# Head-major cumulated decays in DRAM, and the substitution's initial values loaded ahead of the diagonal blocks

## The chip, the cores and the metric

The kernel runs on one core of a Trainium2 chip. The metric is the device time of one launch in microseconds (us), the median of three runs. All engines of the core work side by side: TensorE (PE, with its weight loads as PEld), VectorE (DVE), ScalarE (ACT), GpSimd (POOL) and SyncE (SP), which here issues all DMA transfers, in one queue in order.

## What is computed

One decoder layer for a sequence of S = 1024 rows of D = 1024 columns, in float32: a gated delta rule with 8 heads and sparse attention in parallel, merged, then an MLP. The change touches the delta rule. Per head, with a chunk of 64 rows (cut from the reference):

```python
g_cum = jnp.cumsum(g, axis=-1)                      # g: log decay, <= 0
diff = g_cum[..., :, None] - g_cum[..., None, :]
decay = jnp.where(incl, jnp.exp(jnp.where(incl, diff, 0.0)), 0.0)
k_beta = k * beta[..., None]
a_mat = jnp.where(strict, jnp.einsum('bhnid,bhnjd->bhnij', k_beta, k) * decay, 0.0)
lhs = a_mat + jnp.eye(C, dtype=f32)
sol = lax.linalg.triangular_solve(lhs, rhs, left_side=True, lower=True, unit_diagonal=True)
...
o = ... lax.scan(step, state0, xs)                  # state carried over the chunks
...
o_gdn = rms_norm(o_gdn, gdn_norm_g) * silu(z)
```

The kernel takes chunks of 128 rows, 8 of them (b = 0 to 7), and inverts each chunk's unit lower triangle of 128 x 128: diagonal blocks of 32 x 32 by substitution, then joins of blocks to 64 and to 128.

## The kernel before

**The planner.** The program is written as many small chains (generators). An object of class `Weave` runs them: it keeps an estimate of when each engine comes free, takes at every step the chain of the best priority that is ready by that estimate, and lets it issue up to its next `yield`. A chain can yield a named event, as `("zu", 3)`, and is not taken up before another chain has announced it. What is issued is fixed: `wv.issue` ties each instruction to the one issued before it on its engine. So the order on each engine is decided by estimates when the program is built, and on the chip every engine works through its own order, with waits where data are late. The time on the chip doesn't feed back into the order. All instructions are recorded by one helper, so the profile gives them all line 2105 (2106 after the change); they are told apart by the names of their tiles.

**The stage of the heads**, from 270 to 980 us. `gdense` (priority 9, the last) computes the projections of the heads' q, k, v and of the gates in units of 128 columns: for each of two halves 24 matmuls `dd` of 128x512 in three passes, so 48 to a unit. These dd are what fills PE between the heads' own work. The first dd of a unit's half waits for the event `("drained", u - 1, half)`: the unit before must have been copied out of PSUM. For a q, k or v that is done by `conv(u)`, the causal convolution, with ACT's copy into `cu` (two buffers); and `conv(u)` waits until the convolution before the last one is done:

```python
if len(convs) > 1:
    yield ("conv", convs[-2])
...
A_.activation(cu[:, 3 + half * HALF:3 + (half + 1) * HALF], cus[u, half], AF.Copy)
wv.done("drained", u, half)
```

A convolution is one product on ACT, three on DVE (`qt<-cu,vecs,qt`), ACT's `cu<-qt` and a last product on DVE (`qt<-cu,qt`).

**A head h** then goes through these chains:
- `keys(h)`: es, the cumulated decays of the head, is read from the DRAM tile GC into all 128 partitions; PE transposes kt (`tt<-ident,kt`); ACT makes `es` = exp(−|es − own decay|); PE multiplies kt with itself, DVE makes the triangle `am`.
- Then, still in `keys`: four stores bring am's diagonal blocks to DRAM (`ZA<-am`), four loads bring them back in another layout into `um` (`um<-ZA`); `sx` is loaded with the initial values `c_xinit`, after the event `("zu", h - 1)` because sx has one buffer; POOL runs 31 steps of substitution, two operations each (`stmp<-sx,um` and `sx<-sx,stmp`); four stores (`ZU<-sx`) and four loads (`um<-ZU`) put the inverses into um, and between them stands `wv.done("zu", h)`.
- `join(h)`: DVE transposes blocks (`t<-um`), PE makes small products of 32 x 32 and 64 x 64 (`jj`), ACT copies between them (`ys`, `t`, `y`, `um`).
- `scan(h)`: over the chunks PE's `cc` and `oo`, DVE's `sr`, `sst` and `vv<-oo`, ACT's `svn`.
- `output(h)`: DVE's small operations on `fe`, `fo`, `fot` (a reciprocal root), `vv<-vv,fo`, PE's `tt<-ident,vv`, a product with the gate, a store.

Meanwhile DVE and ACT count for the attention's selection of keys (`tkeq`, `tkcm`, with `cand` and `thr`). Behind the heads the attention opens: SP loads `ql`, PE transposes it (`s<-ident,ql`), ACT and DVE split it into `qh` and `qlo`, PE makes the scores (`s<-kTh,qh` and the like). `misc_post`, ahead of the stage, computes the cumulated decays gc and stores them to GC.

Of the kernel before, what the change touches and what calls it, by code (L numbers as in the profile page):

```python
# [9 lines left out]
F32 = mybir.dt.float32  # L10
# [10 lines left out]
P = 128  # L21
S = 1024
D = 1024
NB = S // P
KT = D // P
HALF = 512
H = 8
# [22 lines left out]
def body(tc, a, out, dbg=None):  # L50
# [4 lines left out]
    def pool(name, bufs=1, side=None, space=None):  # L55
        kw = {}
        if space is not None:
            kw["space"] = space
        elif side is not None:
            kw["side"] = side  # L60
        if space is not DRAM:
            kw["reuse_waits"] = "tile"
        es = ExitStack()
        p = es.enter_context(tc.tile_pool(name=name, bufs=bufs, **kw))
        return p, es
# [16 lines left out]
    dr, dr_es = pool("dr", space=DRAM)  # L82
# [15 lines left out]
    V_, A_, G_, PE_, SY_ = (wv.engine(e, n) for e, n in ((V, "V"), (A, "A"), (G, "G"), (PE, "PE"), (SY, "SY")))  # L98
# [21 lines left out]
    ident = cst.tile([P, P], F32, name="ident")  # L120
# [20 lines left out]
    kng = ix.tile([P, P], F32, name="kng")  # L141
    QD = dr.tile([S, H * P], F32, name="QD")
    KD = dr.tile([S, 2 * P], F32, name="KD")
    GC = dr.tile([H * NB, P], F32, name="GC")
    XD = dr.tile([S, D], F32, name="XD")
    VD = dr.tile([S, 2 * P], F32, name="VD")
    xs, vrow = [], scp.tile([P, P], F32, name="tkcm")
# [135 lines left out]
    def dense():  # L283
        jobs = [(0, 0), (1, 0), (0, 1), (1, 1), (1, 2)]
        jobs += [(u, t) for u in range(2, len(units)) for t in range(3 if u == 2 else 4)]
        for u, t2 in jobs:
# [3 lines left out]
            if u == 0:  # L290
                if t2 == 0:
                    outs[u] = ix.tile([P, S], F32, name="misc")
                    wv.add(1, misc_post())
                ps = pd.tile([P, HALF], F32, name="dd")
                n = 0
                for k in range(KT):
                    yield ("ht", t2, k)
                    h_, l_ = hi[k], lo[k]
                    for l, r in ((h_, ht_hi[k][t2]), (h_, ht_lo[k][t2]), (l_, ht_hi[k][t2])):
                        PE_.matmul(ps, l, r, start=n == 0, stop=n == 3 * KT - 1)  # L300
                        n += 1
                        yield 0.0
                wv.add(1, drain(outs[u][:, t2 * HALF:(t2 + 1) * HALF], ps, ("half", t2)))
                if t2:
                    wv.done("pdense", u)
                continue
# [46 lines left out]
    def col(name, pl=cst):  # L353
        return pl.tile([P, NB, H], F32, name=name)

    c64 = lambda t: t.rearrange("p b h -> p (b h)")
    gx, gt, gu, gl_, gd = (col(n, ix) for n in ("gx", "gt", "gu", "gl_", "gd"))
    aexp = cst.tile([P, H], F32, name="aexp")
    beta = col("beta")
    gc, ngc, eg, egl, egd = (col(n) for n in ("gc", "ngc", "eg", "egl", "egd"))  # L360
# [4 lines left out]
    def misc_post():  # L365
# [59 lines left out]
        pg = p1.tile([P, 4, P], F32, name="tp")  # L425
        PE_.matmul(pg[:, 0, :64], triu, c64(gl_), start=True, stop=True)
        PE_.matmul(pg[:, 1, :64], ones, c64(gl_), start=True, stop=True)
        yield
        V_.tensor_copy(c64(gc), pg[:, 0, :64])
        V_.tensor_scalar(c64(ngc), pg[:, 0, :64], -1.0, None, op0=OP.mult)  # L430
        A_.activation(c64(egl), pg[:, 1, :64], AF.Exp)
        yield
# [2 lines left out]
        yield  # L435
        A_.activation(egd, egd, AF.Exp)
        pg = p1.tile([P, 4, P], F32, name="tp")
        PE_.transpose(pg[:64, 0, :], c64(gc), ident)
        yield
        gr = ix.tile([64, P], F32, name="gt")  # L440
        V_.tensor_copy(gr, pg[:64, 0, :])
        yield
        SY_.dma_start(GC, gr)


    scores = {qb: mkp.tile([P, (qb + 1) * P], F32, name=f"sc{qb}") for qb in range(2, NB)}
# [309 lines left out]
    def conv(u):  # L756
# [35 lines left out]
        wv.done("conv", u)  # L792
        st[h][c + "t"] = o
        wv.add(2, {"k": keys, "q": queries, "v": values}[c](h))


    def keys(h):
# [4 lines left out]
        es = gp.tile([P, NB, P], F32, name="es", bufs=2)  # L802
        am = gq.tile([P, NB, P], F32, name="am", bufs=2)
        um = gp.tile([P, NB, P], F32, name="um", bufs=2)
        kss = gp.tile([P, NB], F32, name="kss", bufs=2)
        SY_.dma_start(es, GC.rearrange("(b h o) p -> h o b p", h=H, o=1)[h].to_broadcast([P, NB, P]))
        dma = ("es", h)
        after(dma)
        for half in range(2):
# [5 lines left out]
            for i in range(4):  # L815
                b = half * 4 + i
# [28 lines left out]
        for half in range(2):  # L845
            yield tt.ready
            ps, slot_ = tt.get()
            for i in range(4):
                b = half * 4 + i
                PE_.matmul(ps[:, i, :], blk(kt, b), blk(kt, b), start=True, stop=True)  # L850
            yield
            for i in range(4):
                b = half * 4 + i
# [10 lines left out]
        st[h].update(kd=kd, aq=es, am=am, av=av, nb=nb_, um=um)  # L864
        wv.done("keys", h)

        for q in range(4):
            SY_.dma_start(ZA[h][:, q].rearrange("n r c -> r n c"),
                          am[32 * q:32 * q + 32, :, 32 * q:32 * q + 32])
        yield  # L870
        sa = um.rearrange("p n c -> p (n c)").rearrange("p (r c) -> p r c", r=32)
        for r in range(4):
            SY_.dma_start(sa[32 * r:32 * r + 32], ZA[h].rearrange("n q r c -> (n q) r c"))
        sx = gq.tile([P, 8, 32], F32, name="sx", bufs=1)
        stmp = gq.tile([P, 8, 32], F32, name="stmp", bufs=1)
        if h:
            yield ("zu", h - 1)
        SY_.dma_start(sx, a["c_xinit"])
        yield
        for j in range(31):  # L880
            w, m = j // 4 + 1, 31 - j
# [9 lines left out]
        zu = ZU[h].rearrange("(n q) k r c -> q (k r) n c", q=4)  # L891
# [205 lines left out]
    gq, gq_es = pool("gq", side="right")  # L1097
# [1079 lines left out]
```

## Time and profile before

| | |
|---|---|
| median of 3 runs | 1871.73 us (1867.83 to 1872.14) |
| the profiled execution | 1870.41 us, its span 1868.7 us |
| mean granted TensorE clock | 0.985 of full speed |
| busy: PE, PEld | 1819.1 us (97%), 1548.2 us (83%) |
| busy: DVE, ACT, POOL | 1261.8 us (68%), 1026.4 us (55%), 531.7 us (28%) |

The profile is one execution, read by the hardware profiler; all durations below are from it. Busy PE is matmuls only, and its ends are modelled, since matmuls overlap in the array; the distance from one start to the next is the better measure. The granted clock is given as a share of the full 2.4 GHz: 0.50 is the lower level of 1.2 GHz, and a figure between them is a mean over a stretch with both. An idle time behind an instruction names its releaser: what the instruction had waited for last.

### The profile page before, as it was taken

How to read it: one execution, taken by the hardware profiler on the slowest of the kernel's cores; microseconds unless marked ns; L12 is line 12 of the kernel's file. 1: busy time of each engine (PE TensorE's matmuls, PEld its weight loads, DVE VectorE, ACT ScalarE, POOL GpSimd, SP SyncE). 2: the span in 40 equal slices, each digit the busy share in tenths (PEclk: the TensorE clock that was granted, in tenths of full speed). 3: DMA queues.
4: the chain of work that ended last, by engine and by line, in shares of the span. 5: the costliest groups of instructions: out<-in, count | busy, mean ns of one | idle time of the engine just before them, and what ended most of it. 6: DMA issues, size and time to landing. Idle time of an engine off the chain costs nothing.

```text
span 1868.7 us, 28344 instructions
## 1 busy us (share of the span) xinstructions
PE 1819.1 (97%) x10214; PEld 1548.2 (83%) x10214; DVE 1261.8 (68%) x2606; ACT 1026.4 (55%) x2262; POOL 531.7 (28%) x751
## 2 busy tenths in 40 slices
PE   8999999999999979999999999999999999999999
PEld 7889998887888868888887788877888888888887
DVE  4557758767768797654347767677766667957655
ACT  6556647756664544553236666666766665333330
POOL 0223640650543146154003211131232222222210
PEclk8999999998999989999999999999999999999999
DMA  4102232312332222222327322221544549463323
GB/s 160 46 25 67 69 114 62 83 44 63 53 79 48 55 67 72 66 63 66 99 95 237 121 80 68 80 96 63 203 158 141 167 160 343 140 198 102 124 79 135
DMA packets 197822, 195.70 MB, mean 105 GB/s; under 512 B 36609, under 2 KB 148658, under 8 KB 197682
## 3 DMA queue, kind: packets, MB, share of 16 engines
q1 hardware_dynamic: 197682, 193.89, 33.8%
q8 instruction: 80, 1.31, 0.3%
q14 instruction: 60, 0.49, 0.1%
HBM read 139.69 MB, written 54.17 MB: 104 GB/s over the span
## 4 chain that ended last, share of the span: by engine, by line
PE 91%; DVE 5%; ACT 3%; DMA 1%; issue 1%; SPq 0%; POOL 0%; DVEq 0%; ACTq 0%; POOLq 0%
PE dd L2105 53%; PE o L2105 15%; PE s L2105 7%; PE pt L2105 6%; PE tt L2105 3%; PE cc L2105 2%; PE jj L2105 2%; PE sq L2105 2%; PE oo L2105 1%; DVE w L2105 1%; DVE rqs L2105 1%; DVE pr L2105 1%; PE tp L2105 0%; DVE sc L2105 0%; DMA pj<-in_x_dram 0%
## 5 line engine op out<-in xcount | busy, mean ns | idle before, releaser
L2105 PE MATMUL dd<-hh,w 128*128 128x512 f32 x1568 | 522.4, 404 | 2.4 <-ACT cu L2105 1.5
L2105 PEld LDWEIGHTS dd<-hh,w 128*128 128x128 f32 x1568 | 292.1, 190 | 55.5 <-ACT cu L2105 2.2
L2105 PE MATMUL dd<-hl,w 128*128 128x512 f32 x784 | 317.2, 405 | 0.6 <-DVE hl L2105 0.6
L2105 PE MATMUL dd<-w,hh 128*128 128x256 f32 x960 | 182.4, 287 | 0.0
L2105 ACT ACTIVATE m<-m 128x512 f32<-128x512 f32 (+1 forms) x240 | 139.8, 624 | 74.5 <-PE dd L2105 31.5
L2105 PE MATMUL dd<-hh,m 128*128 128x512 f32 x520 | 172.1, 396 | 1.9 <-DVE w L2105 1.6
L2105 PEld LDWEIGHTS dd<-hl,w 128*128 128x128 f32 x784 | 149.2, 190 | 26.8 <-DVE hl L2105 1.5
L2105 DVE TENSOR_TENSOR m<-m,m 128x512 fp32r<-128x512 f32 (+2 forms) x177 | 134.8, 789 | 36.2 <-ACT m L2105 32.7
L2105 PEld LDWEIGHTS dd<-w,hh 128*128 128x128 f32 x960 | 154.4, 194 | 1.6
L2105 POOL TENSOR_TENSOR stmp<-sx,um 128x60 f32<-128x60 f32 (+24 forms) x248 | 111.8, 451 | 98.1 <-DMA sx<-in_c_xinit_dram 79.9
L2105 PE MATMUL dd<-w,hl 128*128 128x256 f32 x480 | 137.3, 286 | 0.0
L2105 PEld LDWEIGHTS dd<-hh,m 128*128 128x128 f32 x520 | 97.1, 189 | 22.0 <-DVE w L2105 1.8
L2105 DVE TENSOR_SCALAR_CACHE_REDUCE tkeq<-sc,cand 128x384 f16<-128x384 f32 (+3 forms) x128 | 103.4, 808 | 1.5
L2105 POOL TENSOR_TENSOR m<-m,m 128x512 f32<-128x512 f32 x48 | 67.6, 1415 | 126.7 <-ACT m L2105 63.3
L2105 PE MATMUL dd<-hl,m 128*128 128x512 f32 x260 | 102.5, 394 | 0.0
L2105 POOL TENSOR_TENSOR sx<-sx,stmp 128x60 f32<-128x60 f32 (+24 forms) x248 | 96.8, 390 | 19.4
L2105 PEld LDWEIGHTS dd<-w,hl 128*128 128x128 f32 x480 | 93.1, 194 | 0.1
L2105 ACT ACTIVATE ha<-m 128x1024 fp32r<-128x1024 f32 x43 | 43.8, 1055 | 80.0 <-PE s L2105 33.8
L2105 DVE TENSOR_TENSOR w<-w,w 128x1024 fp32r<-128x1024 f32 (+1 forms) x56 | 64.7, 1160 | 25.8 <-ACT w L2105 25.6
L2105 ACT ACTIVATE hh<-m 128x1024 fp32r<-128x1024 f32 x40 | 40.7, 1054 | 75.1 <-PE o L2105 37.6
L2105 PE MATMUL o<-hh,m 128*128 128x512 f32 x248 | 80.3, 391 | 0.0
L2105 ACT ACTIVATE tkcm<-sc,cand 128x896 f16<-128x896 f32 x64 | 69.9, 1093 | 17.4 <-DVE cand L2105 12.9
(460 smaller groups left out, 4427.5 us busy)
## 6 DMA issues: line engine op xcount, KB each, us to landing
HD<-m SPq DMA_DIRECT2D x106, 256.0 KB, 2.3
m<-HD SPq DMA_DIRECT2D x53, 512.0 KB, 3.9
w<-in_w_in_dram SPq DMA_DIRECT2D x48, 512.0 KB, 3.9
m<-in_w_mlp_up_dram SPq DMA_DIRECT2D x33, 512.0 KB, 5.0
wraw<-in_w_in_dram SPq DMA_DIRECT2D x8, 1024.0 KB, 5.2
m<-in_w_mlp_down_dram SPq DMA_DIRECT2D x16, 512.0 KB, 4.5
w<-in_x_dram SPq DMA_DIRECT2D x10, 512.0 KB, 4.7
hh<-in_w_mlp_down_dram SPq DMA_DIRECT2D x10, 512.0 KB, 5.0
```

Of the source, the lines that this page charges most:

```text
L2105: ins = f(*args, **kw)
```

## The change

Two edits. The DRAM tile GC gets a row of 1024 numbers for each head, where it had a row of 128 for each pair of chunk and head. For that gc is copied once more on DVE, into `gx` with the heads outermost, gx is transposed instead of gc, and the store goes to the new layout. A head's es is then read as one piece of 4 KB for each partition, where it was eight of 512 B. In `keys`, the wait for `("zu", h - 1)` and the load of sx now stand ahead of the ZA stores and the um loads; so these too come behind `("zu", h - 1)`.

```diff
--- before.py
+++ after.py
@@ -141,7 +141,7 @@
     kng = ix.tile([P, P], F32, name="kng")
     QD = dr.tile([S, H * P], F32, name="QD")
     KD = dr.tile([S, 2 * P], F32, name="KD")
-    GC = dr.tile([H * NB, P], F32, name="GC")
+    GC = dr.tile([H, S], F32, name="GC")
     XD = dr.tile([S, D], F32, name="XD")
     VD = dr.tile([S, 2 * P], F32, name="VD")
     xs, vrow = [], scp.tile([P, P], F32, name="tkcm")
@@ -427,6 +427,7 @@
         PE_.matmul(pg[:, 1, :64], ones, c64(gl_), start=True, stop=True)
         yield
         V_.tensor_copy(c64(gc), pg[:, 0, :64])
+        V_.tensor_copy(c64(gx).rearrange("p (h b) -> p b h", h=H), pg[:, 0, :64].rearrange("p (b h) -> p b h", h=H))
         V_.tensor_scalar(c64(ngc), pg[:, 0, :64], -1.0, None, op0=OP.mult)
         A_.activation(c64(egl), pg[:, 1, :64], AF.Exp)
         yield
@@ -435,12 +436,12 @@
         yield
         A_.activation(egd, egd, AF.Exp)
         pg = p1.tile([P, 4, P], F32, name="tp")
-        PE_.transpose(pg[:64, 0, :], c64(gc), ident)
+        PE_.transpose(pg[:64, 0, :], c64(gx), ident)
         yield
         gr = ix.tile([64, P], F32, name="gt")
         V_.tensor_copy(gr, pg[:64, 0, :])
         yield
-        SY_.dma_start(GC, gr)
+        SY_.dma_start(GC.rearrange("h (b p) -> (h b) p", p=P), gr)
 
 
     scores = {qb: mkp.tile([P, (qb + 1) * P], F32, name=f"sc{qb}") for qb in range(2, NB)}
@@ -803,7 +804,7 @@
         am = gq.tile([P, NB, P], F32, name="am", bufs=2)
         um = gp.tile([P, NB, P], F32, name="um", bufs=2)
         kss = gp.tile([P, NB], F32, name="kss", bufs=2)
-        SY_.dma_start(es, GC.rearrange("(b h o) p -> h o b p", h=H, o=1)[h].to_broadcast([P, NB, P]))
+        SY_.dma_start(es.rearrange("p b c -> p (b c)"), GC[h:h + 1, :].to_broadcast([P, S]))
         dma = ("es", h)
         after(dma)
         for half in range(2):
@@ -864,18 +865,18 @@
         st[h].update(kd=kd, aq=es, am=am, av=av, nb=nb_, um=um)
         wv.done("keys", h)
 
-        for q in range(4):
-            SY_.dma_start(ZA[h][:, q].rearrange("n r c -> r n c"),
-                          am[32 * q:32 * q + 32, :, 32 * q:32 * q + 32])
-        yield
-        sa = um.rearrange("p n c -> p (n c)").rearrange("p (r c) -> p r c", r=32)
-        for r in range(4):
-            SY_.dma_start(sa[32 * r:32 * r + 32], ZA[h].rearrange("n q r c -> (n q) r c"))
         sx = gq.tile([P, 8, 32], F32, name="sx", bufs=1)
         stmp = gq.tile([P, 8, 32], F32, name="stmp", bufs=1)
         if h:
             yield ("zu", h - 1)
         SY_.dma_start(sx, a["c_xinit"])
+        for q in range(4):
+            SY_.dma_start(ZA[h][:, q].rearrange("n r c -> r n c"),
+                          am[32 * q:32 * q + 32, :, 32 * q:32 * q + 32])
+        yield
+        sa = um.rearrange("p n c -> p (n c)").rearrange("p (r c) -> p r c", r=32)
+        for r in range(4):
+            SY_.dma_start(sa[32 * r:32 * r + 32], ZA[h].rearrange("n q r c -> (n q) r c"))
         yield
         for j in range(31):
             w, m = j // 4 + 1, 31 - j
```

The count of every kind of instruction on every engine stays the same, but for one DVE copy more. The orders of all engines are alike up to the heads' stage at about 387 us, and again from the attention's later part on (about 1290 us); between, the planner has set them anew. On SP, head 1 went before: ZA(1), a weight load, um<-ZA(1), ZU(0), a weight load, um<-ZU(0), sx; after: ZU(0), a weight load, um<-ZU(0), sx, ZA(1), um<-ZA(1), and ZU(1) comes one weight load later. Three places are shown, on PE and once on DVE.

**The unit boundary at 613 us.** The names dd<-hh and dd<-hl are the dense matmuls; a new second name behind them (w_6543 and w_6544, then w_6718) marks the next unit. Before, on PE:

```order
L2105 MATMUL dd<-hh_110,w_6544 128x512
L2105 MATMUL dd<-hh_112,w_6543 128x512
L2105 MATMUL dd<-hl_113,w_6543 128x512
L2105 MATMUL dd<-hh_112,w_6544 128x512
L2105 MATMUL jj<-um,am 64x64 x8
L2105 MATMUL tt<-ident,kt 128x128 x4
L2105 MATMUL jj<-y_6911,t_6786 64x64 x8
L2105 MATMUL cc<-vv,um 128x128
L2105 MATMUL cc<-svn,kd 128x128
L2105 MATMUL oo<-svn,es 128x128
L2105 MATMUL tt<-ident,vv 128x128 x4
L2105 MATMUL dd<-hh_98,w_6718 128x512
```

After; the last oo of the scan of head 2 stands four rows above these:

```order
L2106 MATMUL dd<-hh_110,w_6489 128x512
L2106 MATMUL dd<-hh_112,w_6488 128x512
L2106 MATMUL tt<-ident,kt 128x128 x4
L2106 MATMUL dd<-hl_113,w_6488 128x512
L2106 MATMUL dd<-hh_112,w_6489 128x512
L2106 MATMUL tt<-ident,kt 128x128 x4
L2106 MATMUL tt<-ident,vv 128x128 x4
L2106 MATMUL jj<-um,am 32x32 x16
L2106 MATMUL tt<-ident,vv 128x128 x4
L2106 MATMUL jj<-ys,t_6886 32x32 x16
L2106 MATMUL jj<-t_6886,ys 32x32 x8
L2106 MATMUL dd<-hh_98,w_6654 128x512
```

Before, 21 dd lay between the end of that scan and the boundary, where the pile of joins, scan and transposes stands; after, 7 lie there, and the pile is 4 groups of transposes and 40 joins. What DVE has to do in the same time begins after the change with these rows, of which the first is that scan's last `vv<-oo`:

```order
L2106 TENSOR_TENSOR vv<-oo,sqs 128x128
L2106 TENSOR_SCALAR tkeq,cnt<-sc_141,cand 128x512
L2106 TENSOR_TENSOR nxt<-nxt,thr 128x1
L2106 TENSOR_SCALAR fe<-qss 128x8
L2106 TENSOR_SCALAR tkeq,cnt<-sc_142,cand 128x640
L2106 TENSOR_TENSOR nxt<-nxt,tki 128x1
L2106 SCALAR_TENSOR_TENSOR fe<-oss,fe 128x8
L2106 TENSOR_SCALAR tkeq,cnt<-sc_143,cand 128x768
L2106 TENSOR_TENSOR thr<-thr,nxt 128x1
L2106 TENSOR_SCALAR fo<-fe 128x8
L2106 TENSOR_SCALAR tki<-cnt 128x4
L2106 SCALAR_TENSOR_TENSOR qt<-cu,vecs,qt 128x1024
```

Behind them follow, in the same order of DVE, one product of w, two more `qt<-cu,vecs,qt`, the other small fo and fot, `vv<-vv,fo`, a memset, three transposes `t<-um`, one `kt<-tt` and `qt<-cu,qt`. Moved ahead of the last product are the memset, the transposes and the `kt<-tt`; the count over 384 columns, which came behind `vv<-oo` before, now stands ahead of it.

**The unit boundary at 655 to 668 us**, the end of the scan of head 3 (a `cc`, `oo` each for the state and for the new values). Before, on PE:

```order
L2105 MATMUL cc<-svn,kd 128x128
L2105 MATMUL oo<-svn,es 128x128
L2105 MATMUL dd<-hh_112,w_6927 128x512
L2105 MATMUL cc<-sst,kt 128x128
L2105 MATMUL oo<-sst,qt 128x128
L2105 MATMUL cc<-sr,um 128x128
L2105 MATMUL oo<-svn,es 128x128
L2105 MATMUL tt<-ident,kt 128x128 x8
L2105 MATMUL tt<-ident,vv 128x128 x4
L2105 MATMUL dd<-hh_98,w_7174 128x512
L2105 MATMUL dd<-hl_99,w_7174 128x512
L2105 MATMUL tt<-ident,vv 128x128 x4
```

After, the same boundary, where w_7193 ends and w_7376 begins; the scan of head 3 is under way here:

```order
L2106 MATMUL oo<-svn,es 128x128
L2106 MATMUL dd<-hl_111,w_7193 128x512
L2106 MATMUL dd<-hh_110,w_7194 128x512
L2106 MATMUL dd<-hh_112,w_7193 128x512
L2106 MATMUL dd<-hl_113,w_7193 128x512
L2106 MATMUL dd<-hh_112,w_7194 128x512
L2106 MATMUL dd<-hh_98,w_7376 128x512
L2106 MATMUL tt<-ident,kt 128x128 x4
L2106 MATMUL dd<-hl_99,w_7376 128x512
L2106 MATMUL dd<-hh_98,w_7377 128x512
L2106 MATMUL dd<-hh_100,w_7376 128x512
L2106 MATMUL dd<-hl_101,w_7376 128x512
```

Before, two rounds of the scan, eight transposes of kt and four of vv stand with no dd between them. After, dd stand between all rows of the scan, its last oo comes 43 dd behind this boundary, and the first transposes of vv another 58 dd behind that.

**The opening of the attention at 982 us.** Before, on PE:

```order
L2105 MATMUL dd<-hl_105,w_10601 128x512
L2105 MATMUL dd<-hh_104,w_10602 128x512
L2105 MATMUL s<-ident,ql 128x128 x4
L2105 MATMUL dd<-hh_106,w_10601 128x512
L2105 MATMUL dd<-hl_107,w_10601 128x512
L2105 MATMUL dd<-hh_106,w_10602 128x512
L2105 MATMUL dd<-hh_108,w_10601 128x512
L2105 MATMUL dd<-hl_109,w_10601 128x512
```

After:

```order
L2106 MATMUL dd<-hh_112,w_10545 128x512
L2106 MATMUL dd<-hl_113,w_10545 128x512
L2106 MATMUL dd<-hh_112,w_10546 128x512
L2106 MATMUL s<-ident,ql 128x128 x4
L2106 MATMUL s<-kTh_10327,qh 128x256
L2106 MATMUL s<-kTl_10329,qh 128x256
L2106 MATMUL s<-kTh_10327,qlo 128x256
L2106 MATMUL s<-kTh_10327,qh 128x256
L2106 MATMUL s<-kTl_10329,qh 128x256
L2106 MATMUL s<-kTh_10327,qlo 128x256
```

Before, 36 dd of the last dense unit followed the first transposes of ql, spread over the opening's first scores; after, the first transposes of ql come behind the last dd.

## Rows read from the trace of the kernel before

**Rows 1.** The page's part 4, the chain that ended last, shares by engine.

```profile
PE 91%; DVE 5%; ACT 3%; DMA 1%; issue 1%; SPq 0%; POOL 0%; DVEq 0%; ACTq 0%; POOLq 0%
```

**Rows 2.** Busy time by stretches; behind each engine its instructions; then clock, DMA share, GB/s.

```profile
449.00:465.00 16.00, 12.94 (x75) 10.49 (x73) 13.66 (x47) 14.34 (x39) 0.10 (x1) 0.68 0.21 67
610.00:625.00 15.00, 11.98 (x64) 10.19 (x65) 11.97 (x31) 10.76 (x35) 0.10 (x1) 0.77 0.23 72
650.00:675.00 25.00, 14.37 (x66) 11.27 (x65) 20.25 (x46) 15.26 (x50) 21.51 (x47) 0.73 0.23 64
675.00:980.00 305.00, 304.94 (x1943) 257.27 (x1942) 168.46 (x355) 131.48 (x371) 92.00 (x214) 1.00 0.28 76
982.00:996.00 14.00, 14.00 (x82) 12.15 (x81) 7.92 (x40) 7.89 (x25) 2.79 (x2) 1.00 0.67 200
996.00:1015.00 19.00, 15.03 (x61) 10.43 (x60) 14.38 (x42) 12.83 (x23) 4.83 (x4) 0.91 0.89 314
```

**Rows 3.** What PE waited for, 440 to 520 us: total, times, longest.

```profile
PE jj L2105 <- ACT y L2105: 1.4, 1, 1.4
PE dd L2105 <- ACT cu L2105: 0.9, 1, 0.9
```

**Rows 4.** What PE waited for, 600 to 710 us.

```profile
PE tt L2105 <- DVE vv L2105: 7.4, 1, 7.4
PE cc L2105 <- DVE sr L2105: 2.4, 1, 2.4
PE cc L2105 <- ACT svn L2105: 1.6, 1, 1.6
...
PE dd L2105 <- ACT cu L2105: 0.5, 1, 0.5
```

**Rows 5.** DVE's groups from 601.2 to 615.1 us: busy, mean ns, idle before.

```profile
L2105 DVE SCALAR_TENSOR_TENSOR qt<-cu,vecs,qt 128x1024 f32<-128x1024 f32 x3 | 3.8, 1282 | 1.4 <-ACT qt L2105 1.4
L2105 DVE TENSOR_SCALAR_CACHE_REDUCE tkeq<-sc,cand 128x384 f16<-128x384 f32 (+3 forms) x4 | 3.2, 810 | 0.0
...
L2105 DVE TENSOR_TENSOR vv<-vv,fo 128x1024 f32<-128x1024 f32 x1 | 1.2, 1224 | 0.0
```

**Rows 6.** Timeline of DVE: start, duration, instruction, idle before it and its releaser.

```profile
599.74 1.31 DVE L2105 STREAM_TRANSPOSE t<-um 32x256 f32<-32x256 f32 x3
...
601.22 0.28 DVE L2105 TENSOR_TENSOR vv<-oo,sqs 128x128 f32<-128x128 f32 x1
...
615.02 1.23 DVE L2105 SCALAR_TENSOR_TENSOR qt<-cu,qt 128x1024 f32<-128x1024 f32 x1 [0.49 <-ACT cu L2105]
```

**Rows 7.** Timeline of PE in three places (joins, head 2, attention's opening).

```profile
447.84 0.91 PE L2105 MATMUL jj<-ys,t 32*32 32x32 f32 x27
...
609.90 0.66 PE L2105 MATMUL tt<-ident,kt 128*128 128x128 f32 x4
...
616.93 0.80 PE L2105 MATMUL dd<-hh,w 128*128 128x512 f32 x1
...
982.64 0.60 PE L2105 MATMUL s<-ident,ql 128*128 128x128 f32 x4
...
989.34 0.39 PE L2105 MATMUL dd<-hl,w 128*128 128x512 f32 x1
...
990.03 0.40 PE L2105 MATMUL dd<-hl,w 128*128 128x512 f32 x1
...
1010.67 0.63 PE L2105 MATMUL dd<-hh,m 128*128 128x512 f32 x1
```

**Rows 8.** The page's part 6, DMA issues: count, KB each, median us to landing.

```profile
es<-GC SPq DMA_DIRECT2D x8, 512.0 KB, 9.1
...
M<-kt SPq DMA_DIRECT2D x8, 512.0 KB, 2.7
...
ZA<-am SPq DMA_DIRECT2D x32, 32.0 KB, 1.6
```

**Rows 9.** What POOL waited for, whole span.

```profile
POOL stmp L2105 <- DMA sx<-in_c_xinit_dram: 79.9, 8, 16.3
```

More of the change, by code (lines that the diff above doesn't have):

```diff
@@ L865, in keys @@
         wv.done("keys", h)
+        sx = gq.tile([P, 8, 32], F32, name="sx", bufs=1)
+        stmp = gq.tile([P, 8, 32], F32, name="stmp", bufs=1)
+        if h:
+            yield ("zu", h - 1)
+        SY_.dma_start(sx, a["c_xinit"])
         for q in range(4):
@@ L873, in keys @@
             SY_.dma_start(sa[32 * r:32 * r + 32], ZA[h].rearrange("n q r c -> (n q) r c"))
[L874 to L878, printed above, removed]
         yield
```

## The prediction

> **What bounds the kernel now.** The chain of work that ended last was read first: 91% of it is TensorE [rows 1]. So time is won or lost only where PE stands idle or runs at the lower of its two clock levels, and every edit is priced by what it does there. The next view was PE by stretches. The change reaches the stage of the recurrent heads (270 to 980 us) and the opening of the attention behind it. From 675 to 980 us PE works 304.94 of 305 us at a granted clock of 1.00 [rows 2]: nothing can be gained there, whatever gets faster. Four stretches lose time [rows 2], and the text calls them A (449 to 465 us), B (610 to 625), C (650 to 675) and D (996 to 1015).
>
> What they cost is worked out in one way. Idle is the width less the busy time. The time at 1.2 GHz is twice the width times what the clock lacks to 1.00; half of the work done in it is lost besides, and the waits that lie in it are taken off first.
> - A: idle 3.1; at half clock 2 x 0.32 x 16 = 10.2, less a wait of 0.9 [rows 3], half of 9.3 is 4.7. Together 7.8 us.
> - B: idle 3.0; at half clock 6.9, less a wait of 1.6 [rows 4], half is 2.7. Together 5.7.
> - C: idle 10.6; at half clock 13.5, less waits of 7.4 and 0.5 [rows 4], half is 2.8. Together 13.4.
> - D: idle 4.0; at half clock 2 x 0.09 x 19 = 3.4, half is 1.7. Together 5.7.
>
> A to C make 27 us: all that any edit can win in the heads' stage. The waits of PE there name the releasers [rows 3, 4]: in C the transposes of a head's output wait 7.4 us for DVE's vv, and the scan of head 3 waits 2.4 us for DVE's sr. No row names the broadcast of the decays or the initial values.
>
> **The transfers themselves: 0.** A head's es load lands 9.1 us after its issue, while 512 KB from kt to M lands in 2.7 [rows 8]; the change makes es look more like the second, perhaps 6 us sooner per head. But a gain on PE needs PE to wait for es's consumers. The substitution on POOL waits 79.9 us in all, 10 a head, for the initial values sx [rows 9]; it gets some of this back; in exchange the ZA stores (1.6 us to landing [rows 8]) and the um loads now stand behind the end of the previous head's substitution. PE's waits that could hang on that road are 1.4 us for y in A [rows 3] and less than the 3.0 idle of B. The dense matmuls dd cover the rest: 304.94 of 305 us. The Trainium skill (Perfetto Trace Analysis, DMA Optimizations) says that transfers under 2 KB carry much overhead and that batching them into 4 or 8 KB can raise throughput a lot. By that rule alone the es load is the gain of this change; the trace agrees on the duration as far as the two rows go, but shows nobody on the path who waits. If the cover were gone, 6 us a head or 48 in all would be at stake; that is excluded, since the idle of A to C together is 16.7.
>
> The added DVE copy of 128x64 is less than a quarter of a microsecond (a 128x128 product took 0.28 [rows 6]) and lies in front of the stage, under dense matmuls: 0, at most 0.3.
>
> **The order: the real content.** Each engine's order is fixed by the planner's estimates, so moving one wait and nine loads and stores reorders every engine from the join of head 1 on. The work is the same to the instruction, so I count what stands between the last dd of a dense unit and the first of the next. The first dd of a unit waits until the PSUM tiles of the unit before are emptied, which waits for a convolution (its last product, then ACT); work that the planner put exactly there has no filler.
>
> *C goes.* Before, the end of scan 3, the transposes of kt and the first of vv all stand at one unit boundary with no dd between them; this is where PE waits 2.4 and 7.4 us [rows 4]. After, dd stand between all of these, and the first transposes of vv of head 3 have 58 dd behind the end of the scan. Three dd take 0.69 us [rows 7], 58 take 13.3; PE waited 7.4 at this place with nothing but eight transposes ahead. So −13.4; at the least −8, should the wait for sr and a half clock stay.
>
> *B grows.* After, only 7 dd follow the last oo of scan 2; then come four groups of transposes and 40 joins with nothing between. PE has in hand 7 x 0.23 = 1.6, four groups at 0.5 = 2.0 (0.66 with the drain), and 40 joins about 2.6 (27 records span 0.91, and a join leaves two): 6.2 us [rows 7]. DVE has to go from the last vv<-oo through four counts (3.2), three taps of the convolution (3.8), a product of w, the small ones of the norm and the vv product (1.2) [rows 5], and then, which is new here, a memset and three transposes (1.3 [rows 6]) ahead of the convolution's last product. Before, from vv<-oo to that last product went 13.8 us, 1.9 of it waiting [rows 5, 6], so 11.9 of work; one count less, the narrowest of four of 0.8 on average, is −0.6, memset, transposes and a kt product of half the width add 2.4: 13.7. From that product to the first dd it took 1.9 [rows 6, 7]. That makes 15.6 without those waits, 17.5 with them. I take 15.8, since ACT's operations now stand earlier relative to DVE's. PE then idles 15.8 − 6.2 = 9.6, nearly as long as in C, and I give it C's loss of clock: 9.6 + 2.8 = 12.4 against 5.7, **+6.7** (+5 to +9).
>
> *A stays.* Before, the joins, transposes and first scan products of the pile fill part of the wait. After, only 40 joins stand at the boundary, 2.6 us, but the convolution's DVE operations stand two places of 1.2 us earlier, so by estimate dd return about 2.5 us sooner. The gap between dd should be 7.0 us, 4.4 of it idle for 3.1, with a shorter time at half clock: **+0.5** (−2 to +3). Head 1 is the one whose substitution the change delays, since its ZA transfers now follow the reload of head 0 on SP; if its um lands behind the place of its join, A goes to its high end.
>
> *D loses its filler.* Before, 36 dd (8.3 us) lie between the opening's first transposes at 982.64 [rows 7] and about 996; after, all dd are done when the opening begins. PE's own work there is 28.0 − 4.0 − 8.3 = 15.7 us (982.64 to the first dd of the next product at 1010.67 [rows 7], idle 4.0). Bounds: if the chain of ACT, DVE and loads is shorter than that work, nothing is lost, or 1 us gained; if it already set the 28 us, all 8.3 are lost, with another 1.1 of clock: 9.4. From 996 to 1010.67, where no filler stands even now, 4.0 of 14.7 us are idle, 27%. The same share on the other 5.0 us of work makes 1.9 us of idle, and a dip of the clock about 1: **+3** (−1 to +9.4).
>
> **Sum:** +0.5 + 6.7 − 13.4 + 3 = −3.2. The profiled execution took 1870.4, so 1867.2; the median of the three runs lies 1.3 above it, so **1868.5 us**. All terms at their low end (C at −13.4) give −11.4; all at their high end (C at −8) +13.4.
>
> **The rivals.**
> - *The pile is dissolved and the opening is not hurt* (faster). B at +5, D at −1, A at 0: −9.4, 1862 us. For it: DVE has spare time in both stretches (20 of 25 us busy in C). Against: DVE's work behind vv<-oo is counted in rows and can't start before it. Chance 0.30, with A below 0 down to 1858.
> - *The opening was set by its chain* (slower). If the road from the loads over ACT and DVE to the scores sets the length of D already, the 8.3 us of filler come back as idle time. D at +9.4: sum +3.2, 1875 us; it turns the sign from D +6.2 on, and with B at its high end it reaches 1877 to 1880. For it: PE waits for ACT, DVE there though it had filler. Against: from 982 to 996 PE works 14.00 of 14 us [rows 2], so nothing there is late by more than the filler is long. Chance 0.24.
> - *The change does what its parts say, and nothing else:* the waits of 1.4 in A and some 1.3 in B on the road of the substitution go, the rest cancels. 1868 to 1870, not to be told from my forecast in time, but in the trace. Chance 0.08.
>
> **How the numbers follow.** The forecast itself has 0.38. A measurement of this kernel tells a change from none at about 0.3%, 5.6 us. Faster by more (below 1866.1): the first rival and a little of the forecast's spread, 0.32. Slower by more (above 1877.3): most of the second, with orders that I have misread, 0.23. The same: 0.45. The range for 8 in 10 takes the first rival's low end and the second's high end: 1858 to 1880.
>
> **What would show it.** Right: C's waits gone and PE above 49 of 50 us from 650 to 700; at the boundary before the first join of head 3 one wait of nearly 10 us, with the clock at 0.50 behind it; D with waits of 5 to 6 us and no dd. es landing in under 6 us and POOL's wait for sx below 80 us would show that the transfers did what they should and that it was hidden. Wrong: a wait of PE for um or am (head 1's road), a B under 5 us, or new waits between 675 and 980 us, where I expect none.

## The result, and the profile after

The changed kernel takes 1880.74 us (median of 4 runs, 1879.08 to 1881.29) against 1869.78 for the kernel before in the same session: a ratio of 1.0058 with a 95% interval of 1.0046 to 1.0071. It is slower by 11 us. Forecast were 1868.5, with a range from 1858 to 1880 and a chance of 0.23 for slower; the measured time lies just above the range.

The profiled execution is the quickest of the four and has a span of 1877.4 us, 8.7 longer than the one shown of before; so the traces account for 8.7 of the 11 us, and the other 2.3 are the distance of the two profiled executions from their medians. The chain that ended last is still PE's, at 92%. So the same reading as before tells where the time went: PE's idle time and half clock, stretch by stretch. These are the stretches that answer to [rows 2], with one more at the start and two from 845 us on (busy time of each engine, then clock, DMA share, GB/s); from 675 to 845 us PE works 169.53 of 170 us:

```profile
160.00:170.00 10.00, 8.03 (x48) 7.60 (x47) 8.19 (x13) 3.57 (x5) 7.99 (x10) 0.83 0.09 31
449.00:465.00 16.00, 10.66 (x111) 8.71 (x107) 9.21 (x25) 12.28 (x33) 0.10 (x1) 0.68 0.13 34
603.00:632.00 29.00, 20.59 (x167) 16.56 (x167) 23.24 (x74) 16.79 (x51) 0.10 (x1) 0.71 0.22 65
650.00:675.00 25.00, 25.00 (x137) 21.36 (x136) 18.19 (x41) 9.77 (x28) 20.89 (x55) 1.00 0.17 46
845.00:862.00 17.00, 12.35 (x83) 9.92 (x81) 11.29 (x31) 8.07 (x23) 0.63 (x1) 0.90 0.43 114
862.00:980.00 118.00, 118.00 (x775) 100.04 (x774) 38.57 (x94) 43.80 (x125) 25.18 (x65) 1.00 0.28 83
991.00:1023.00 32.00, 23.25 (x109) 16.76 (x108) 23.03 (x79) 20.21 (x46) 10.08 (x7) 0.95 0.79 264
```

What PE waited for from 440 to 1025 us (total, times, longest):

```profile
PE tt L2106 <- DVE vv L2106: 8.4, 1, 8.4
PE jj L2106 <- ACT ys L2106: 5.2, 1, 5.2
PE dd L2106 <- DVE w L2106: 4.7, 1, 4.7
PE s L2106 <- ACT qh L2106: 4.2, 3, 2.6
PE pt L2106 <- ACT pr L2106: 1.8, 1, 1.8
PE o L2106 <- DVE pl L2106: 1.2, 1, 1.2
```

The losses of the two profiles side by side, worked out as in the prediction (idle, and half of the work done at 1.2 GHz); the forecast's terms stand beside them:

| place | before, us | after, us | difference | forecast |
|---|---|---|---|---|
| start, wait for iqs at 164 us | 1.6 | 3.7 | +2.0 | 0 (at most 0.3) |
| A, 449 to 465 | 7.8 | 8.3 | +0.5 | +0.5 |
| B, 610 (now 603) to 632 | 5.7 | 14.3 | +8.6 | +6.7 (+5 to +9) |
| C, 650 to 675 | 13.4 | 0 | −13.4 | −13.4 |
| small wait at 774 | 0 | 0.5 | +0.5 | none |
| E, 845 to 862 | 0 | 6.4 | +6.4 | none |
| D, attention's opening | 5.7 | 10.4 | +4.7 | +3 (−1 to +9.4) |

The differences add up to 9.3, the spans differ by 8.7. The table can be checked where PE's instructions stand in the same order in both kernels: after the change they start 0.25 us earlier at 150 us, 1.6 later at 175, 1.5 later at 380, and 8.7 later at 1300 us and from there to the end. So all but 1.5 us of the loss arises between 380 and 1300 us, 7.25 us, where the table has 7.3. B's sum reads: idle 29.00 − 20.59 = 8.4; at half clock 2 x 0.29 x 29 = 16.8, less 5 of the wait that lie in it, half is 5.9. The road through it, on DVE and on PE, begins with the last vv<-oo of head 2's scan and ends with the unit's first dd:

```profile
605.55 0.29 DVE L2106 TENSOR_TENSOR vv<-oo,sqs 128x128 f32<-128x128 f32 x1 [0.30 <-PE oo L2106]
...
618.54 1.22 DVE L2106 SCALAR_TENSOR_TENSOR qt<-cu,qt 128x1024 f32<-128x1024 f32 x1
```

```profile
616.42 1.09 PE L2106 MATMUL tt<-ident,vv 128*128 128x128 f32 x4 [8.41 <-DVE vv L2106]
...
622.46 0.80 PE L2106 MATMUL dd<-hh,w 128*128 128x512 f32 x1
```

It takes 16.9 us, 8.5 of them PE's own work; [rows 6, 7] have 15.7 for before, with 21 dd to fill it.

The transfers did what the change says. A head's es load lands in 3.7 us instead of 9.1 [rows 8], and POOL's longest-waited-for transfer is no longer the initial values: 44.8 us for um<-ZA instead of 79.9 for sx [rows 9].

```profile
es<-GC SPq DMA_DIRECT2D x8, 512.0 KB, 3.7
```

```profile
POOL stmp L2106 <- DMA um<-ZA: 44.8, 7, 9.8
```

E is the place that the prediction had not seen. The timeline of PE there (start, duration, instruction, idle before and its releaser):

```profile
847.74 0.60 PE L2106 MATMUL tt<-ident,vv 128*128 128x128 f32 x4
...
849.79 0.60 PE L2106 MATMUL tt<-ident,vv 128*128 128x128 f32 x4
...
850.70 1.05 PE L2106 MATMUL tt<-kt 128*128 128x128 f32 x8
856.40 0.50 PE L2106 MATMUL dd<-hh,w 128*128 128x512 f32 x1 [4.66 <-DVE w L2106]
```

The same on DVE and on ACT:

```profile
848.38 0.75 DVE L2106 SCALAR_TENSOR_TENSOR kt<-tt,g,w 128x512 f32<-128x512 f32 x1 [0.70 <-PE tt L2106]
850.43 0.75 DVE L2106 SCALAR_TENSOR_TENSOR kt<-tt,g,w 128x512 f32<-128x512 f32 x1 [1.30 <-PE tt L2106]
851.75 1.23 DVE L2106 TENSOR_TENSOR w<-w,w 128x1024 fp32r<-128x1024 f32 x1 [0.57 <-PE tt L2106]
...
855.59 0.16 DVE L2106 SCALAR_TENSOR_TENSOR nb<-ck,eg 128x8 f32<-128x8 f32 x1
855.67 0.68 DVE L2106 SCALAR_TENSOR_TENSOR w<-th,dd 128x512 f32<-128x512 f32 x1
```

```profile
850.66 1.06 ACT L2106 ACTIVATE w<-w 128x1024 fp32r<-128x1024 f32 x1 [0.81 <-PE dd L2106]
851.63 0.68 ACT L2106 ACTIVATE es<-es,ngc 128x128 f32<-128x128 f32 x2
852.34 0.63 ACT L2106 ACTIVATE es<-es 128x512 f32<-128x512 f32 x1
852.87 1.07 ACT L2106 ACTIVATE th<-dd 128x512 f32<-128x512 f32 x2
```

The dense unit that ended at 850 is the z gate of head 7. Its drain is ACT's `th<-dd` and DVE's `w<-th,dd`, and in the code it begins only after the output of head 5, with whose gate it shares a buffer:

```python
if c == "z":
    if h > 1:
        yield ("out", h - 2)
    zzs[h] = slot((1, 5)[h % 2], [P, S], F32)
```

The output of head 5 ends with the two `kt<-tt,g,w` at 848 and 850 us. Only behind it does the order on ACT have `th<-dd`, and on DVE `w<-th,dd` stands behind a chain of small operations from 852.9 on. The first dd of the next unit waits for it: 4.7 us idle, then 3.4 us at half clock. Counted in the two traces, 56 dd lay before the change between the last transposes of head 5's output (`tt<-ident,vv`) and the end of this unit; after it there are 2.

### The profile page after: what moved, and what is told of

Read it like the earlier page. It is cut to its first block, busy times and chain, and to the rows that moved or that the text cites. A ratio compares the mean times of both kernels' runs of the same rounds, so it can differ in the third digit from the quotient of the medians.

```text
span 1877.4 us, 28340 instructions
## 1 busy us (share of the span) xinstructions
PE 1820.6 (97%) x10214; PEld 1549.9 (83%) x10214; DVE 1264.0 (67%) x2607; ACT 1028.2 (55%) x2262; POOL 533.0 (28%) x751
## 4 chain that ended last, share of the span: by engine, by line
PE 92%; DVE 4%; ACT 2%; issue 1%; DMA 1%; POOL 0%; SPq 0%; ACTq 0%; DVEq 0%; POOLq 0%
PE dd L2106 53%; PE o L2106 14%; PE s L2106 7%; PE pt L2106 6%; PE tt L2106 3%; PE cc L2106 2%; PE jj L2106 2%; PE sq L2106 2%; PE oo L2106 1%; DVE w L2106 1%; DVE rqs L2106 1%; PE tp L2106 1%; DVE sc L2106 0%; DVE pr L2106 0%; DMA pj<-in_x_dram 0%
## 5 line engine op out<-in xcount | busy, mean ns | idle before, releaser
L2106 POOL TENSOR_TENSOR stmp<-sx,um 128x60 f32<-128x60 f32 (+24 forms) x248 | 108.8, 439 | 63.3 <-DMA um<-ZA 44.8
L2106 POOL TENSOR_TENSOR sx<-sx,stmp 128x60 f32<-128x60 f32 (+24 forms) x248 | 101.4, 409 | 19.4
L2106 ACT ACTIVATE tkcm<-sc,cand 128x896 f16<-128x896 f32 x64 | 70.1, 1095 | 15.8 <-DVE cand L2106 11.9
```

The source lines that it names most:

```text
L2106: ins = f(*args, **kw)
```

## The experiments

Two theories stood against each other. **Theory 1:** the time is made by the order of the engines' instructions, which the planner set anew; the transfers themselves are hidden. **The rival:** the moved transfers act directly, above all the diagonal blocks that now wait for the previous head's substitution. Where a run is said to have an order, PE, DVE and ACT stand in it instruction by instruction in its trace, but for the copy. All ratios are to the kernel before in the same session.

**The first edit alone.** The layout with its copy, and nothing else of the diff.

> Only the first edit: decays head by head in DRAM, with the added copy; the initial values stay where they were before. As built, every engine's order is that of before but for the copy. Theory 1 (the time is made by the order of the engines, and the transfers are hidden): es lands in under 6 us instead of 9.1, no wait of PE changes, 1870 us within 3. Rival (a shorter es load moves the work of the heads): 1860 to 1866, or slower by new collisions.

Measured: 1871.5 us (10 runs), ratio 1.0009 (1.0000 to 1.0019). es lands in 3.7 us, and PE's waits from 440 to 1010 us are those of before, each within 0.4. So 5.4 us less for each head's load gain nothing; the small loss is taken up below.

**The second edit alone.**

> Only the second edit: the wait for the previous head's substitution and the load of the initial values stand ahead of the diagonal blocks' transfers; the decays lie as before. As built, all four compute engines stand in the order of the whole change, but for its copy. Theory 1: the whole effect, 1880 us within 3, with the waits of about 5 us at 455, 8 at 616, 5 at 856 us. Rival: if the layout has a part in it, clearly less than 1880.

Measured: 1879.07 us, ratio 1.0053 (1.0038 to 1.0068): nearly the whole loss, with the waits of B, E and D as in the whole change. A differs in its releaser: with the slow es load ahead of it on SP, um of head 1 lands late, at about 451 us instead of 447.

```profile
PE tt L2105 <- DVE vv L2105: 8.4, 1, 8.4
PE dd L2105 <- DVE w L2105: 4.7, 1, 4.7
PE s L2105 <- ACT qh L2105: 4.2, 3, 2.6
...
PE jj L2105 <- DMA um<-ZU: 3.9, 1, 3.9
```

**Both edits in the transfers, the order of before.** The planner is charged at the old places and the transfers are issued at the new one, without a charge.

```diff
-        for q in range(4):
-            SY_.dma_start(ZA[h][:, q]...)
+        for q in range(4):
+            wv.phantom("SY", 0.5, SY_LATENCY)      # the planner's cost, no instruction
         yield
-        for r in range(4):
-            SY_.dma_start(sa[...], ZA[h]...)
+        for q in range(4):
+            wv.phantom("SY", 0.5, SY_LATENCY)
         if h:
             yield ("zu", h - 1)
         SY_.dma_start(sx, a["c_xinit"])
+        wv.free = True                             # instructions without a cost
+        for q in range(4):
+            SY_.dma_start(ZA[h][:, q]...)
+        for r in range(4):
+            SY_.dma_start(sa[...], ZA[h]...)
+        wv.free = False
```

> Both edits in the transfers, but the planner is given the costs of before, so that PE, DVE, ACT and POOL keep the order of before to the instruction (but for the copy), and only SP's queue differs. Theory 1: 1870 us within 4, waits as before (7.4 us for vv at 667 us). Rival (the diagonal blocks that now wait for the previous head's substitution come late, and the joins with them): waits of PE or DVE for um, above all at head 1, and 1876 to 1882 us.

Measured: 1871.15 us (10 runs), ratio 1.0010 (1.0001 to 1.0020), the same as the layout alone. POOL waits more than before, and PE waits for what it waited for before:

```profile
POOL stmp L2121 <- DMA um<-ZA: 90.9, 8, 16.6
```

```profile
PE tt L2121 <- DVE vv L2121: 7.0, 1, 7.0
PE cc L2121 <- DVE sr L2121: 2.3, 1, 2.3
```

**No edit in the transfers, the order of the change.** The reverse: the transfers are issued as before, the planner is charged as by the change.

> Neither edit in the transfers: decays and diagonal blocks move as before. But the planner is given the costs of the change, so that PE, DVE, ACT and POOL stand in the order of the change (but for its copy). Theory 1: 1880 us within 3, the same waits at 455, 616 and 856 us. Rival (late diagonal blocks): back to about 1870, since the blocks come early again.

Measured: 1878.57 us, ratio 1.0050 (1.0035 to 1.0065), with the change's waits, A's with the releaser that the second edit alone has:

```profile
PE tt L2119 <- DVE vv L2119: 8.4, 1, 8.4
PE dd L2119 <- DVE w L2119: 4.7, 1, 4.7
PE s L2119 <- ACT qh L2119: 4.2, 3, 2.6
PE jj L2119 <- DMA um<-ZU: 3.9, 1, 3.9
```

So the late um of head 1 is not the work of the moved diagonal blocks, which keep their old place here. POOL is done with head 1's substitution at 420 us here (416 in the kernel before), but in the change's order the ZU stores stand on SP behind one weight load more, and that is issued at 436.8 us; in the kernel before, the stores were issued at 422.

These four runs settle the theories. With the order of before the time stays within 2 us whatever the transfers do; with the order of the change it is 9 us longer even where the edited transfers are as before. The order includes that of SP's other transfers, which no run separates from the rest; in the whole change no wait of PE from 440 to 1025 us names a transfer.

**Which head's move sets the order.** The layout, without its copy (below), and the second edit at head 1 alone:

> The layout without the copy, and the second edit at head 1 alone; the other heads wait and load as before. As built, the orders of PE, DVE and ACT are those of the whole change, but for its copy. Theory 1 (the whole loss is the order, and the order turns on head 1): 1878 us within 2, which is the whole change less the 2 us of the copy, with the waits of 8 us at 616 and 5 at 856. Rival (each head's move costs about 1.3 us): 1870 to 1872.

Measured: 1878.87 us, ratio 1.0055 (1.0038 to 1.0072), with the waits of 8.4 and 4.7 us. Then at all heads but 1 and 3, which leaves PE, DVE and ACT in the order of before:

> The layout without the copy, and the second edit at all heads but 1 and 3. As built, PE, DVE and ACT stand in the order of before to the instruction. Theory 1: 1869 us within 2, as the layout alone without its copy; POOL's waits before the substitution are shorter and nobody gains. Rival (six heads whose substitution starts sooner gain something): 1860 to 1866.

Measured: 1870.55 us (10 runs), ratio 1.0006 (0.9997 to 1.0015). Six heads start their substitution with the new order of transfers, and nobody gains or loses. Then from head 2 on, a third order:

> The layout without the copy, and the second edit from head 2 on. As built, this is a third order: as before up to the boundary at 613 us; there a pile of joins with four transposes of vv; at 655 us three scan steps and the transposes of kt without those of vv; dd among the attention's opening. Theory 1: between the two, with the wait for vv of 7 us gone from the boundary at 655 and a longer one at 613: 1862 to 1872. Rival (any order but that of before costs about 10 us): 1877 to 1881.

Measured: 1870.66 us (10 runs), ratio 1.0010 (1.0001 to 1.0019): in the stated range, but its mechanism missed. The wait for vv is gone from C, but the first dd of the unit then waits 9.0 us for the convolution instead, and C loses 13.6 us, as much as before (idle 10.8; at half clock 10.2, less 4.6 of the wait, half is 2.8):

```profile
PE dd L2110 <- ACT cu L2110: 11.5, 3, 9.0
```

```profile
650.00:680.00 30.00, 19.21 (x94) 15.78 (x93) 22.39 (x53) 15.77 (x52) 25.20 (x61) 0.83 0.12 36
```

That is a correction to the way C was read: PE's wait for vv hid another one of nearly the same length behind it, the convolution's, which DVE's work sets as well.

**The new wait E.** The whole change, with a gate unit that needs nothing of the heads drawn ahead of the z gate of head 7:

```diff
     gunits += [(h, "b") for h in range(H)]
+    gunits.insert(gunits.index((7, "z")), gunits.pop(gunits.index((0, "b"))))
```

> The whole change, with one dense unit drawn ahead: a gate unit that needs nothing of the heads stands in front of the z gate of head 7, whose drain waits for the output of head 5. As built, PE's order is that of the change, and DVE and ACT differ in some 20 rows around 850 us. Theory 1a (the wait of 4.7 us at 856 us is the drain of that z gate, held up by a head's output that the change made later against the dense units): the wait goes, with it 1.7 us of half clock, so 1874 us within 2. Rival (the wait is DVE's load of small operations at that place): the wait stays or moves by a unit, 1879 to 1881.

Measured: 1877.18 us (7 runs), ratio 1.0036 (1.0026 to 1.0047): between the two ranges that were stated. E is gone, A, B and D's waits stay. DVE's small operations stand where they stood, from 852.2 us on, with the z gate's `w<-th,dd` behind them, and PE doesn't wait: they alone are not the cause.

```profile
830.00:870.00 40.00, 40.00 (x293) 33.42 (x292) 23.09 (x59) 21.74 (x67) 1.27 (x2) 1.00 0.33 91
991.00:1020.00 29.00, 21.86 (x85) 15.79 (x85) 20.88 (x63) 18.51 (x39) 10.07 (x7) 0.82 0.83 276
```

The time falls by 3.6, not by 6.4. In the attention's opening, which begins at 985 us here, PE idles 9.3 us from 980 to 1030 (8.7 in the change), and the mean clock from 991 to 1020 is 0.82 against 0.95; counted as in the table the opening loses about 14 us for 10.4, so some 3.5 of the 6.4 went there. The profiled execution took 1874.47 us, and its span is 4.7 below that of the change; 1.0 of that is won up to 380 us, where the half clock behind the copy is missing. The seven executions lie apart: three took 1874.3 to 1875.0 us at a mean clock of 0.985 or 0.986, four took 1877.2 to 1879.4 at 0.980 to 0.983.

This run alone doesn't isolate the drain, since in its trace PE's order from 850 to 992 us differs from that of the change, other than the expectation says. What bears the reading out is the count of dd over all the orders. Where 0 or 2 dd lie between the last transposes of head 5's output and the end of the z gate's unit (the paced counts below, and the four kernels with the change's order), the next unit's first dd waits 3.9 to 4.7 us; where 49 to 96 lie there (all others; 51 in this run), it doesn't wait.

**The copy.** The first edit without it; the transpose is that of gc again, and the store sorts the rows:

```diff
-        SY_.dma_start(GC, gr)
+        SY_.dma_start(GC.rearrange("h (b p) -> b h p", p=P), gr)
```

> The first edit without its DVE copy: gc is transposed as before, and the store into the new layout is strided. All compute engines keep the order of before. Theory 1b (the copy delays DVE's chain of the start, so that PE waits 1.97 instead of 1.64 us at 164 us and then runs 3.4 us at half clock): the wait is 1.64 again without a half clock behind it, 1869.6 us, some 2 below the first edit with its copy. Rival (the copy costs nothing, the difference between the starts is chance): no difference to the first edit with its copy, 1871.5.

Measured: 1869.19 us (11 runs), ratio 0.9996 (0.9987 to 1.0005). And the copy alone, in the kernel before, with a result that nobody reads:

> The kernel before with the added DVE copy alone, whose result nobody reads; layout, transfers and orders as before. Theory 1b (the copy itself costs the start 0.3 us of waiting and 1.7 of half clock): PE waits 1.97 us at 164 us, half clock behind it, 1871.5 us, about 2 above before. Rival (it is the store or the transpose of the new layout, not the copy): 1.64 us and 1869.6.

Measured: 1872.18 us (12 runs), ratio 1.0009 (1.0000 to 1.0018). The timelines of PE at the wait, first the layout without the copy, then the copy alone, each with its stretch of 160 to 170 us:

```profile
164.53 0.66 PE L2105 MATMUL tp<-ident,iqs 128*128 128x128 f32 x4 [1.64 <-DVE iqs L2105]
```

```profile
160.00:170.00 10.00, 8.36 (x63) 7.89 (x62) 8.20 (x11) 4.29 (x6) 9.24 (x11) 1.00 0.01 3
```

```profile
165.82 0.44 PE L2115 MATMUL tp<-ident,iqs 128*128 128x128 f32 x2 [1.96 <-DVE iqs L2115]
```

```profile
160.00:170.00 10.00, 8.04 (x53) 7.69 (x52) 8.32 (x9) 2.53 (x4) 9.61 (x9) 0.83 0.00 0
```

All profiles with the copy have a wait of 1.96 or 1.97 us here, all others one of 1.64; behind it the clock is at half for 3.4 us in four profiles of five with the copy (in the one of the moved gate unit it is not), and in none without. So the copy of 0.27 us comes with 0.3 us of waiting each time, and mostly with 1.7 of clock. The ratios alone (1.0009 for the copy and for the layout with it, 0.9996 for the layout without it) would hardly show it, since the intervals of the first two begin at 1.0000.

The 0.3 us are not the copy's own time, handed on. From 111 to 150 us PE, DVE and ACT keep one distance to the kernel before (0.25 us earlier in the changed kernel). At the same row of DVE this distance then grows by 0.32 or 0.33 in all five profiles with the copy, and in none of those without; before the change, and after:

```profile
150.70 0.89 DVE L2105 SCALAR_TENSOR_TENSOR sc<-irl,iw,sc 128x640 f32<-128x640 f32 x1
```

```profile
150.78 0.89 DVE L2106 SCALAR_TENSOR_TENSOR sc<-irl,iw,sc 128x640 f32<-128x640 f32 x1 [0.40 <-ACT irl L2106]
```

The `irl` that is named as releaser had ended at 150.42 us, so what DVE waits for there, 77 us behind the copy, stays open.

**Order alone.** To see what an order is worth, the kernel before with nothing changed but the planner's estimate of a transfer's latency, 2.2 or 2.8 us instead of 2.5:

> The kernel before; only the planner's estimate of a transfer's latency is 2.2 us instead of 2.5, so that the same instructions stand in another order. Theory 1 (order alone moves the time by as much as the change did): a difference of 3 us or more to 1869.6 in either direction, all of it in waits of PE and the half clock behind them at other places than before. Rival (the order matters only where transfers move): within 2 us of 1869.6.

Measured: 1880.8 us, ratio 1.0049 (1.0032 to 1.0066).

> The same with 2.8 us. Theory 1: again a difference of 3 us or more to 1869.6, and another one than with 2.2. Rival: within 2 us of 1869.6.

Measured: 1878.83 us, ratio 1.0044 (1.0030 to 1.0058). In both, C is gone and other waits have come: with 2.2 a wait of 4.3 us for um of head 3 at B, with 2.8 waits for ACT's t and ys and for mx in D.

```profile
PE jj L2105 <- DMA um<-ZU: 4.3, 1, 4.3
```

```profile
PE jj L2105 <- ACT t L2105: 4.9, 3, 2.3
PE s L2105 <- DVE mx L2105: 3.8, 2, 3.6
```

That they are different from each other, the expectation of the second run, is not clear from 2 us.

**A version that should be faster.** The kernel before with the selection's counts spread, so that DVE has fewer of them where the piles stand:

```diff
-            yield 8.0
+            yield 10.0
```

> The kernel before, with the attention's counts for the selection of keys paced at one round each 10 us instead of 8, so that DVE has fewer of them beside the heads up to 680 us and more behind, where PE never waits. As built, no pile stands at the boundary at 655 us, piles stand at those at 450 and 613, and dd stand in the attention's opening. Theory 2 (the piles cost what DVE has to do in them, and the counts are 3 us of each): 1858 to 1867. Rival (a new order is as good as drawn, whatever is taken off DVE): anywhere from 1869 to 1882.

Measured: 1873.44 us (10 runs), ratio 1.0018 (1.0009 to 1.0028): the rival. C is gone, B loses 10.2 us for 5.7, E turns up here too, 3.9 us at 852, and in the attention's opening, with 12 dd behind the first transposes of ql instead of 36, PE idles 8.3 us for 4.0.

```profile
PE dd L2105 <- DVE w L2105: 3.9, 1, 3.9
```

No version beat the kernel before; the layout without its copy equals it.

## Why the prediction was wrong

**Right, by step.** That the transfers are worth nothing: es 5.4 us sooner per head, POOL's waits otherwise, and within 2 us no effect with the order held. The Trainium skill's advice (Perfetto Trace Analysis, DMA Optimizations) to batch pieces under 2 KB holds here for the duration, 3.7 us for 9.1; nobody on the path waits for it. That the order is the content of the change. C at −13.4, with PE at 25.00 of 25 us; that a second wait, the convolution's, stood behind the one for vv was not seen, and the change happened to dissolve both. A at +0.5, by luck: its wait is another (ACT's ys, where the order has counts and es ahead of it), and 5.3 us of idle time where 4.4 were put in meet 3.0 of clock where the sum implies 3.9. B at +8.6 for +6.7, inside its bounds and with the wait that was forecast.

**The step that failed** is the way of counting: "I count what stands between the last dd of a dense unit and the first of the next", and with it the expectation of no new waits between 675 and 980 us, where PE worked 304.94 of 305 us before. The prediction itself named such waits as a sign of being wrong. At E only eight transposes, 1.05 us, stand between the two dd on PE. What holds the second is a drain that waits for a head's output, by an event in the code and not by a row of PE's order. The change's order has the end of head 5's output 54 dd later against the dense units, so that it now comes where the z gate of head 7 wants to drain. The full stretch of before showed that nothing could be gained, not that nothing could be lost. E is 6.4 of the 12.5 us between the forecast's sum (−3.2) and the table's (+9.3). That the wait is the gate's drain is read from the code and the three timelines; the count of dd over all orders agrees with it, and so does the run with the unit drawn ahead.

**The terms that were mis-sized:** the copy, "0, at most 0.3", measured 2.0 in the profile and about 1.7 in the ratio of the copy alone. It was priced by its length and its cover; what came with it is a wait of DVE 77 us behind it, and the half clock behind PE's longer wait. B, 1.9 over, all of it clock: its idle time is 8.4 us for the 9.6 put in, since the road took 16.9 instead of 15.8 but PE's own work on it 8.5 instead of 6.2; the clock costs 5.9, where C's 2.8 was put in. The opening D, +3, measured +4.7: 8.7 us of idle time for 4.0, with the clock's part as before. That the lost filler is the cause was argued from the order and no run isolates it, but the orders agree: PE's idle time in the 40 us from the first transposes of ql is 2.7, 4.0, 6.6, 7.3, 8.3 and 8.7 us where 47, 36, 20, 17, 12 and 0 dd are left behind them (moved from head 2 on, before, latency 2.2, latency 2.8, paced counts, the change).

**The rivals.** The slower one named the opening alone, up to 1875 to 1880; the opening had a part of 4.7, E and B more. The late um of head 1, given as A's high end, occurs (3.9 us in the run with the second edit alone), but not for the reason given: it comes as well where the ZA transfers keep their place, from the place of the ZU stores on SP and the slow es. With the quick es um lands at 447.2 us, 1.2 ahead of the first joins.

What stays open: why the opening loses more once E is gone, what DVE waits for at 150.8 us in the kernels with the copy, and which of the moved rows a better order would have to put elsewhere.

## What to carry to other kernels

Where a planner fixes the order, a change has two effects that are to be costed apart: what the moved work does in the old order, and what the new order does with the old work; both can be built, by charging the planner for one and issuing the other, and here the second was everything. Reorderings of the same instructions gave 1869 to 1881 us, so an order alone can be worth some 10 us, and a gain below that from any edit upstream has to be measured with the order held. In reading a new order, follow every event that a buffer's release waits for, not only what stands in the rows of the bounding engine; and a stretch in which that engine is full can still lose.

## What the runs showed of the hardware

A copy of 0.27 us on an engine that is busy 68% of the span came with a loss of about 2: DVE waits 0.40 us at a row 77 us behind it, in all five profiles with the copy and in none of ten without, and one wait of PE grows from 1.64 to 1.96 us. Behind the longer wait TensorE ran at 1.2 GHz for 3.4 us in four of five profiles, behind the shorter one in none. And one DMA of 512 KB into 128 partitions landed in 3.7 us as one piece of 4 KB per partition where eight of 512 B took 9.1, while the weight loads of the same size with pieces of 512 B landed in 3.9: the size of the piece alone does not explain the 9.1. What does was not tried.
